# Context modulation dot products on three engines, and the second layer's gate dot products made in the second layer

## The chip, the cores and the metric

The kernel runs on one core of one Trainium2 chip. A core has a matrix engine (PE, with its weight loads shown as PEld), a vector engine (DVE), a scalar engine (ACT), a general-purpose engine (POOL) and a queue that issues the transfers (SP). Each engine takes its own instructions in the order in which the program lists them, and waits on semaphores for the others. The metric is the device time of one execution in microseconds; lower is better. About 0.3% (4.4 us) is what a measurement of this kernel can tell from no change.

## The reference

Two layers work on 1024 latent tokens and 256 context tokens of width 1024. Ahead of each layer a conditioning vector gives three vectors per token kind (shift, scale, gate), by a product with a weight matrix; the latent tokens use `c`, the context tokens use `c_ctx`:

```python
silu_c, silu_cc = silu(c), silu(c_ctx)
for i in range(2):
    shift, scale, gate = split(silu_c @ w_ada[i] + b_ada[i], 3)
    shift_c, scale_c, gate_c = split(silu_cc @ w_ada[i] + b_ada[i], 3)
    u = h * (1 + scale) + shift            # context: uc with shift_c, scale_c
    y, yc = mixer_a(u, uc) if i == 0 else mixer_b(u, uc)
    h = layer_norm(alpha * h + gate * y)   # context: hc with gate_c, first layer only
```

`mixer_a` is windowed attention of 16 heads with a sink and a SiLU gate path; `mixer_b` is a neighbourhood attention of 16 heads with a learned bias. All is float32. The context's output of the second layer is not needed, so the second layer's `gate_c` is never used.

## The kernel before

**Matrix products.** To keep float32 accuracy, every operand is split into a high part (a rounded copy, made on ACT) and a low part (the rest, made on DVE or POOL), and each product is three matmuls (L207 to L209). Weights of 128x512 come in by transfers (L149), ACT copies the high part (L163), and POOL or DVE makes the low part (L165).

**First layer, about 120 to 610 us.** The attention is cut into 160 sub-blocks (head pair p of 8, query block b of 10, head h of 2). One sub-block goes through these steps. PE makes the scores S_A (L685, L686). DVE adds the mask and takes the row maximum: s_A (L315). POOL copies the sink into one more column (L320). ACT takes the exponential and its row sum (L322). DVE inverts the sum: rs_A (L326). POOL multiplies by it (L327). PE transposes: T_A (L334). ACT copies the high part: pth_A (L338). DVE makes the low part: ptl_A (L340). PE multiplies with the values: pvA (L714). The scores run three sub-blocks ahead of the transposes. Scores and transposes take turns in the same two PSUM buffers (`big`), so PE can write the next one only when DVE has read the one that stands there: T_A waits for s_A, S_A waits for ptl_A.

Between these steps PE does the projections of the next head pair (gate and query), laid in by `merge`. Their results leave PSUM through `g_evac` (ACT L275, DVE L276) and `rope_evac` with `q_store` (DVE L463, L464, POOL L465, DVE L466, ACT L640, DVE L641). A head pair is called a unit below; the rope work falls in the second half of a unit, in its query blocks 6 to 9 (its tail), the earlier ones are its head.

**The dot products.** The modulation of the first layer's gate and of the whole second layer is 32 columns of 128 outputs, and for each the vector `silu(c)` (v=0) and, for the first 24 columns, `silu(c_ctx)` (v=1) has to be multiplied with 128 rows of `w_ada` and summed. This is spread over the first layer's attention. `dot_half(h, j)` (from L584) handles one half of the 1024 terms of column j: it loads 128x512 of `wadaT` (L597) and gives DVE a multiply-and-sum with v=1 (L600, if j < 24) and one with v=0 (L601). There are 64 such steps, laid into units 0 to 6 by `SEG` (9 or 10 a unit, every seventh item of a unit's list). With their second instruction, which reads the sum out, they are 112 dot products on DVE. `dots_end` (L604) adds the halves and the bias and forms `colA`, `colB` for the second layer's input.

**Second layer, from about 640 us.** Projections run first; the attention of 16 heads begins at 823 us, with the steps of the first layer (L1016 and L1017 for S_B, L315, L322, L326, L327, L334, L338, L340). Heads are stored to and loaded from DRAM by SP (L906, L915, L967, L972). The second layer's gate (columns 24 to 31) is used only after the attention, by `gate_rows`.

**What sets the order.** The code is recorded once; a list scheduler then places each instruction on its engine by modelled times and priorities (`tc.high_priority` lifts the attention's steps). The order on an engine can thus differ from the order in the code. Once placed, an engine never takes a later instruction ahead of one that waits.

Of the kernel before, what the change touches and what calls it, by code (L numbers as in the profile page):

```python
# [11 lines left out]
F32 = mybir.dt.float32  # L12
# [3 lines left out]
ALU = mybir.AluOpType  # L16
# [3 lines left out]
P = 128  # L20
# [17 lines left out]

SDOTS = (1, 3)

SEG = (9, 9, 9, 9, 9, 9, 10, 0)


def f32(ap):
# [38 lines left out]
def build(tc, i, out):  # L83
# [494 lines left out]
    dma(msk, i["maskA"])  # L578


    dhalf = cp.tile([P, 32, 2], F32, name="dhalf")
    gh = []

    def dot_half(h, j):  # L584
        def run():
            if j == 0:
                gh.clear()
                for v in range(2):
                    t = px.tile([P, 512], F32, tag=f"gh{v}", bufs=1, name="gh")
                    dma(t, bass.AP(i["cr"].tensor, v * D + h * 512, [[0, P], [1, 512]]))  # L590
                    th = px.tile([P, 512], F32, tag="gw", bufs=2, name="gth")
                    nc.scalar.activation(th, t, AF.Tanh, scale=0.5)
                    nc.vector.scalar_tensor_tensor(t, th, 1.0, t, ALU.add, ALU.mult)
                    gh.append(t)
            acc = dhalf if h else dcol
            t = px.tile([P, 512], F32, tag="gw", bufs=2, name="gw")
            dma(t, i["wadaT"][j, :, h * 512 : (h + 1) * 512])  # L597
            if j < 24:
                o = ap_.tile([P, 512], F32, tag="ra", bufs=1, name="gj")
                nc.vector.tensor_tensor_reduce(o, t, gh[1], 0.5, 0.0, ALU.mult, ALU.add, accum_out=acc[:, j, 1:2])  # L600
            nc.vector.tensor_tensor_reduce(t, t, gh[0], 0.5, 0.0, ALU.mult, ALU.add, accum_out=acc[:, j, 0:1])  # L601

        return (0.0, run, 0)

    def dots_end():
        for v in range(2):
            n = 24 if v else 32
            d = dcol[:, 0:n, v]
            nc.vector.tensor_tensor(d, d, dhalf[:, 0:n, v], ALU.add)
            nc.vector.tensor_tensor(d, d, bad[:, 16 : 16 + n], ALU.add)  # L610
            shift, scale = dcol[:, 8:16, v], dcol[:, 16:24, v]
            nc.vector.scalar_tensor_tensor(colA[:, v, :], scale, 1.0, lnc[:, 0, :], ALU.add, ALU.mult)
            nc.vector.scalar_tensor_tensor(colB[:, v, :], scale, 1.0, lnc[:, 1, :], ALU.add, ALU.mult)
            nc.vector.tensor_tensor(colB[:, v, :], colB[:, v, :], shift, ALU.add)

    dots = [dot_half(h, j) for h in range(2) for j in range(32)]
    evs = []
    for c, (t0, n) in enumerate(CHUNKS):
        for nt in range(2):
# [469 lines left out]
    e_load(0)  # L1089
    bias_make(0)  # L1090
    e_load(1)
    attB = [(0.0, start_B, kqv_done[0])]
    last = 0
    for n, row in enumerate(rowsB):
        ex = []
        if n < len(subsB):
            h, jp, r = subsB[n]
            if h == 14 and jp == 0 and r == 0:
                last = len(attB)
            if h + 1 < NH and r == 0:  # L1100
# [181 lines left out]
```

## Time and profile before

| what | before |
|---|---|
| median of 3 runs (lowest, highest) | 1473.45 us (1472.22, 1476.23) |
| the profiled execution | 1476.44 us, of which the span from first to last instruction is 1474.7 us |
| PE busy over the span | 1401.7 us (95%) |
| DVE busy | 1048.1 us (71%) |
| ACT busy | 715.9 us (49%) |
| POOL busy | 620.1 us (42%) |
| mean granted TensorE clock | 0.983 |

The span stands 1.7 us below the profiled execution's own time, and that execution is 3.0 us above the median. A share over the whole span hides the stages: DVE is near full in the first layer and about half full in the second, so the prediction reads the stretches apart. PE's busy time is modelled and counts overlapping matmuls once; what matters is where PE stands idle and for whom.

### The profile page before, as it was taken

What the parts mean: (1) busy time and instruction counts of PE and PEld (TensorE: products, weight loads), DVE (VectorE), ACT (ScalarE), POOL (GpSimd) and SP (SyncE); (2) the same over time, 40 slices, a digit from 0 to 9 for tenths busy, and PEclk for the clock granted to TensorE, in tenths of its full rate; (3) what the DMA queues carried; (4) which work ended last, traced back from release to release, by engine and by line L of the source; (5) the groups of instructions that cost most, each with busy time, mean ns of one, the idle gap of its engine ahead of it and who ended that gap; (6) DMA issues with size and microseconds to landing.
All of it is one profiled execution on the core that took longest, in us unless ns stands there. A gap on an engine that the chain in (4) does not pass through costs nothing.

```text
span 1474.7 us, 24806 instructions
## 1 busy us (share of the span) xinstructions
PE 1401.7 (95%) x8660; PEld 1231.5 (84%) x8660; DVE 1048.1 (71%) x2339; ACT 715.9 (49%) x1481; POOL 620.1 (42%) x739
## 2 busy tenths in 40 slices
PE   7898999999999999999999999999999999998995
PEld 5797888888888788878888889888998899877784
DVE  6957999988998988666632565655565555677788
ACT  4525566666666668633222444554454444457300
POOL 3433655555655546423311232332233323345564
PEclk6999999999999999999999999999999999999998
DMA  8455222311412213333267355555555465564443
GB/s 308 160 191 149 65 90 80 122 62 54 134 45 75 90 49 119 115 128 131 91 191 209 95 162 153 151 171 140 163 159 162 131 177 150 143 191 123 140 118 91
DMA packets 117084, 194.51 MB, mean 132 GB/s; under 512 B 9312, under 2 KB 57824, under 8 KB 116960
## 3 DMA queue, kind: packets, MB, share of 16 engines
q1 hardware_dynamic: 116960, 192.92, 43.7%
q8 instruction: 69, 1.13, 0.3%
q14 instruction: 55, 0.45, 0.1%
HBM read 140.98 MB, written 51.90 MB: 131 GB/s over the span
## 4 chain that ended last, share of the span: by engine, by line
PE 62%; DVE 19%; issue 6%; ACT 5%; DMA 4%; POOL 3%; SPq 0%; DVEq 0%; ACTq 0%; POOLq 0%
PE pj L207 8%; PE pj L209 8%; PE pj L208 8%; PE T_B L334 4%; PE pvB L1047 4%; DVE s_A L315 3%; PE T_A L334 3%; DVE ptl_A L340 3%; PE pv L240 3%; PE pv L241 3%; PE pv L242 3%; PE S_B L1016 3%; PE yA L419 2%; PE yA L417 2%; PE yA L418 2%
## 5 line engine op out<-in xcount | busy, mean ns | idle before, releaser
L327 POOL TENSOR_SCALAR s_B<-s_B,rs_B 128x640 f32<-128x640 f32 (+1 forms) x128 | 101.6, 794 | 304.0 <-DVE rs_B L326 281.2
L207 PE MATMUL pj<-uBh,wh 128*128 128x512 f32 (+1 forms) x448 | 176.2, 393 | 0.0
L322 ACT ACTIVATE s_A<-s_A,m_A 128x641 f32<-128x641 f32 (+2 forms) x160 | 119.6, 747 | 116.7 <-DVE m_A L315 94.8
L208 PE MATMUL pj<-uBl,wh 128*128 128x512 f32 (+1 forms) x448 | 169.5, 378 | 0.0
L209 PE MATMUL pj<-uBh,wl 128*128 128x512 f32 (+1 forms) x448 | 169.4, 378 | 0.0
L327 POOL TENSOR_SCALAR s_A<-s_A,rs_A 128x640 f32<-128x640 f32 (+2 forms) x160 | 137.5, 860 | 73.3 <-DVE rs_A L326 69.6
L340 DVE TENSOR_TENSOR pt_B<-T_B,pt_B 128x640 fp32r<-128x640 f32 (+1 forms) x128 | 101.0, 789 | 84.1 <-ACT pt_B L338 83.7
L322 ACT ACTIVATE s_B<-s_B,m_B 128x640 f32<-128x640 f32 (+1 forms) x128 | 102.9, 804 | 116.2 <-DVE m_B L315 114.8
L207 PE MATMUL pj<-uAh,wh 128*128 128x512 f32 (+1 forms) x384 | 141.6, 369 | 0.0
L315 DVE CUSTOM_DVE_ANT_0 s_A<-S_A,msk,nsk 128x640 f32<-128x640 f32 (+2 forms) x160 | 123.6, 773 | 22.4 <-PE S_A L686 13.7
L209 PE MATMUL pj<-uAh,wl 128*128 128x512 f32 (+1 forms) x384 | 138.3, 360 | 0.0
L208 PE MATMUL pj<-uAl,wh 128*128 128x512 f32 (+1 forms) x384 | 137.7, 359 | 0.0
L165 POOL TENSOR_TENSOR wl<-wr,wh 128x512 fp32r<-128x512 f32 x64 | 88.6, 1386 | 100.4 <-ACT wh L163 94.2
L340 DVE TENSOR_TENSOR ptl_A<-T_A,pth_A 128x640 fp32r<-128x640 f32 (+2 forms) x160 | 113.8, 711 | 6.3 <-ACT pth_A L338 3.8
L338 ACT CAST pt_B<-T_B 128x640 fp32r<-128x640 f32 (+1 forms) x128 | 84.4, 659 | 67.3 <-PE T_B L334 66.7
L334 PE MATMUL T_A<-ident,s_A 128*128 128x128 f32 x672 | 101.3, 275 | 14.0 <-DVE m_A L315 7.4
L334 PEld LDWEIGHTS T_A<-ident,s_A 128*128 128x128 f32 x672 | 78.0, 141 | 40.3 <-issue 15.2
L315 DVE CUSTOM_DVE_ANT_0 s_B<-S_B,bias 128x640 f32<-128x640 f32 (+1 forms) x128 | 100.5, 785 | 10.4 <-PE S_B L1017 9.6
L338 ACT CAST pth_A<-T_A 128x640 fp32r<-128x640 f32 (+2 forms) x160 | 96.7, 604 | 19.4 <-PE T_A L334 16.4
L209 PEld LDWEIGHTS pj<-uBh,wl 128*128 128x128 f32 x448 | 84.2, 188 | 16.7
L334 PE MATMUL T_B<-ident,s_B 128*128 128x128 f32 x608 | 88.1, 274 | 9.9 <-DVE pt_B L340 6.2
L240 PE MATMUL pv<-wh,uBh 128*128 128x256 f32 x320 | 92.1, 288 | 0.9 <-ACT wh L163 0.9
(189 smaller groups left out, 3916.5 us busy)
## 6 DMA issues: line engine op xcount, KB each, us to landing
kB<-kdB SPq DMA_DIRECT2D x64, 320.0 KB, 5.5
gw<-in_wadaT SPq DMA_DIRECT2D x64, 256.0 KB, 2.8
vdB<-st SPq DMA_DIRECT2D x20, 512.0 KB, 3.3
vB<-vdB SPq DMA_DIRECT2D x16, 640.0 KB, 4.6
kdB<-st SPq DMA_DIRECT2D x16, 512.0 KB, 2.9
qdB<-st SPq DMA_DIRECT2D x16, 512.0 KB, 3.3
qB<-qdB SPq DMA_DIRECT2D x32, 256.0 KB, 4.7
ogr<-ogd SPq DMA_DIRECT2D x28, 256.0 KB, 3.0
```

What stands on the lines that cost most here:

```text
L165: e.tensor_tensor(lo, r, f32(hi), ALU.subtract)
L207: mm(pt[:, :n], hi[:, sl], rh, start=kt == 0, stop=False)
L208: mm(pt[:, :n], hi[:, sl], rl, start=False, stop=False)
L209: mm(pt[:, :n], lo[:, sl], rh, start=False, stop=kt == KT - 1)
L240: mm(pt, lh, hi[:, sl], start=kt == 0, stop=False)
L315: nc.vector.tensor_tensor_reduce(outp, sc, in1, scale, init if init is not None else 3e38, ALU.add, ALU.min, accum_out=s.m)
L322: nc.scalar.activation(s.t[:, :n], s.t[:, :n], AF.Exp, bias=s.m, scale=-1.0, accum_out=s.sum)
L327: nc.gpsimd.tensor_scalar(s.t[:, : s.w], s.t[:, : s.w], s.rs, 1.0, ALU.mult, ALU.mult)
L334: nc.tensor.transpose(tp[:, k * P : (k + 1) * P], s.t[:, src * P : (src + 1) * P], ident)
L338: nc.scalar.copy(pt.hi[:, :n, hl, :], tv)
L340: nc.vector.tensor_tensor(pt.lo[:, :n, hl, :], tv, f32(pt.hi[:, :n, hl, :]), ALU.subtract)
L1047: mm(ov[:, :, 1], v[:, t, :], x[:, k], start=not side and k + n == 0, stop=k == 3 and n == 1)
```

## The change

`dot_half` no longer makes columns 24 to 31, so there are 48 steps, and `SEG` lays 7 (in the last unit 6) into a unit. In each step DVE makes the v=0 dot product, POOL makes the product of the v=1 half (new L607, in place in the weight tile), and ACT sums that product over the row. The sum (new L588) is written at the start of the next step's code, by `dot_sum`. The second layer's columns 24 to 31 are loaded (new L1109) and summed on DVE (new L1118) one half at a time in one buffer, `gwB`; the code lists load and dot in turn, one at each second sub-block of heads 0 to 8.

```diff
-SEG = (9, 9, 9, 9, 9, 9, 10, 0)
+SEG = (7, 7, 7, 7, 7, 7, 6, 0)
...
-    dhalf = cp.tile([P, 32, 2], F32, name="dhalf")
-    gh = []
+    dhalf = cp.tile([P, 24, 2], F32, name="dhalf")
+    gh, sums = [], []
+
+    def dot_sum():
+
+        if sums:
+            t, acc = sums.pop()
+            nc.scalar.activation(t, t, AF.Copy, scale=0.5, accum_out=acc)
 
     def dot_half(h, j):
         def run():
+            dot_sum()
             if j == 0:
...
             dma(t, i["wadaT"][j, :, h * 512 : (h + 1) * 512])
-            if j < 24:
-                o = ap_.tile([P, 512], F32, tag="ra", bufs=1, name="gj")
-                nc.vector.tensor_tensor_reduce(o, t, gh[1], 0.5, 0.0, ALU.mult, ALU.add, accum_out=acc[:, j, 1:2])
-            nc.vector.tensor_tensor_reduce(t, t, gh[0], 0.5, 0.0, ALU.mult, ALU.add, accum_out=acc[:, j, 0:1])
+            o = ap_.tile([P, 512], F32, tag="ra", bufs=1, name="gj")
+            nc.vector.tensor_tensor_reduce(o, t, gh[0], 0.5, 0.0, ALU.mult, ALU.add, accum_out=acc[:, j, 0:1])
+            nc.gpsimd.tensor_tensor(t, t, gh[1], ALU.mult)
+            sums.append((t, acc[:, j, 1:2]))
...
     def dots_end():
+        dot_sum()
...
-    dots = [dot_half(h, j) for h in range(2) for j in range(32)]
+    dots = [dot_half(h, j) for h in range(2) for j in range(24)]
...
+    gsil = bp.tile([P, D], F32, name="gsil")
+    gwB = {}
+
+    def gate_load(j, x):
+        gwB[j, x] = bp.tile([P, 512], F32, tag="gwB", bufs=1, name=f"gwB{j}_{x}")
+        if j < 0:
+            if x == 0:
+                dma(gsil, bass.AP(i["cr"].tensor, 0, [[0, P], [1, D]]))
+        else:
+            dma(gwB[j, x], i["wadaT"][24 + j][:, HALVES[x]])
+
+    def gate_dot(j, x):
+        t = gwB.pop((j, x))
+        g, acc = gsil[:, HALVES[x]], dcol[:, 24 + j, 0:1]
+        if j < 0:
+            nc.scalar.activation(t, g, AF.Tanh, scale=0.5)
+            nc.vector.scalar_tensor_tensor(g, t, 1.0, g, ALU.add, ALU.mult)
+            return
+        nc.vector.tensor_tensor_reduce(t, t, g, 0.5, acc if x else 0.0, ALU.mult, ALU.add, accum_out=acc)
+        if j == KT - 1 and x:
+            nc.vector.tensor_tensor(dcol[:, 24:32, 0], dcol[:, 24:32, 0], bad[:, 40:48], ALU.add)
+
...
+            if h <= KT and r == 1:
+                ex.append((0.0, lambda h=h, x=jp // 2, f=gate_dot if jp % 2 else gate_load: f(h - 1, x)))
```

**Place 1: ACT and DVE in unit 1, sub-blocks 27 and 28.** Sub-blocks carry their number in the names (s_A28 is the masked score of sub-block 28), and `gw` is the weight tile of a dot product. On ACT, before:

```order
L322 ACTIVATE s_A27_2141,sum_A27_2143<-s_A27_2141,m_A27_2142 128x641
L338 CAST pth_A24_2126<-T_A25_2166 128x5x128
L163 CAST wh18_2255<-wr18_1862 128x512
L322 ACTIVATE s_A28_2187,sum_A28_2189<-s_A28_2187,m_A28_2188 128x641
L338 CAST pth_A26_2210<-T_A26_2212 128x5x128
```

and on ACT now:

```order
L322 ACTIVATE s_A27_2135,sum_A27_2137<-s_A27_2135,m_A27_2136 128x641
L338 CAST pth_A24_2120<-T_A25_2160 128x5x128
L588 ACTIVATE gw_2172,dcol_73<-gw_2172 128x512
L322 ACTIVATE s_A28_2182,sum_A28_2184<-s_A28_2182,m_A28_2183 128x641
L338 CAST pth_A26_2205<-T_A26_2207 128x5x128
L163 CAST wh18_2250<-wr18_1858 128x512
```

The sum of tile gw_2172 stands on ACT ahead of the exponential of sub-block 28. On DVE, before:

```order
L326 RECIPROCAL rs_A27_2144<-sum_A27_2143 128x1
L600 ISA gj_2179,dcol_73<-gw_2177,gh_1134 128x512
L600 ISA dcol_73 128x1
L315 ISA s_A28_2187,m_A28_2188<-S_A28_2182,msk_145,nsk_146 128x640
L315 ISA m_A28_2188 128x1
L340 TENSOR_TENSOR ptl_A24_2127<-T_A25_2166,pth_A24_2126 128x5x128
L601 ISA gw_2177,dcol_73<-gw_2177,gh_1129 128x512
L601 ISA dcol_73 128x1
L326 RECIPROCAL rs_A28_2190<-sum_A28_2189 128x1
L315 ISA s_A29_2228,m_A29_2229<-S_A29_2223,msk_145,nsk_146 128x640
```

and on DVE now:

```order
L326 RECIPROCAL rs_A27_2138<-sum_A27_2137 128x1
L606 ISA gj_2174,dcol_73<-gw_2172,gh_1129 128x512
L606 ISA dcol_73 128x1
L315 ISA s_A28_2182,m_A28_2183<-S_A28_2177,msk_145,nsk_146 128x640
L315 ISA m_A28_2183 128x1
L340 TENSOR_TENSOR ptl_A24_2121<-T_A25_2160,pth_A24_2120 128x5x128
L326 RECIPROCAL rs_A28_2185<-sum_A28_2184 128x1
L315 ISA s_A29_2223,m_A29_2224<-S_A29_2218,msk_145,nsk_146 128x640
```

One of the two dot products is gone; the other (of the same tile gw_2172 that ACT sums) stands where it stood, between the two reciprocals.

**Place 2: POOL at the same sub-blocks.** Before:

```order
L320 COPY s_A28_2187<-nsk_146 128x1
L327 TENSOR_SCALAR s_A27_2141<-s_A27_2141,rs_A27_2144 128x640
L165 TENSOR_TENSOR wl18_2256<-wr18_1862,wh18_2255 128x512
L320 COPY s_A29_2228<-nsk_146 128x1
L327 TENSOR_SCALAR s_A28_2187<-s_A28_2187,rs_A28_2190 128x640
```

and now:

```order
L320 COPY s_A28_2182<-nsk_146 128x1
L327 TENSOR_SCALAR s_A27_2135<-s_A27_2135,rs_A27_2138 128x640
L607 TENSOR_TENSOR gw_2172<-gw_2172,gh_1134 128x512
L320 COPY s_A29_2223<-nsk_146 128x1
L327 TENSOR_SCALAR s_A28_2182<-s_A28_2182,rs_A28_2185 128x640
```

The product of gw_2172 stands behind the scaling of sub-block 27 and ahead of that of sub-block 28.

**Place 3: DVE and SP at the start of the second layer's attention.** `pj50` and `pj52` are projections of the second head pair, `wr` raw weights, `st` tiles on their way to DRAM, and gwB2_0 is the first half of the third gate column. On DVE, before:

```order
L905 SCALAR_TENSOR_TENSOR st_9208<-pj50_2_9183,st_9208 128x256
L914 TENSOR_TENSOR st_9249<-pj52_0_9224,st_9249 128x512
L165 TENSOR_TENSOR wl57_9287<-wr57_9222,wh57_9286 128x512
L914 TENSOR_TENSOR st_9278<-pj52_1_9253,st_9278 128x512
L315 ISA s_B0_9317,m_B0_9318<-S_B0_9312,bias0_8673 128x512
```

and now:

```order
L912 SCALAR_TENSOR_TENSOR st_9209<-pj50_2_9184,st_9209 128x256
L1118 ISA gwB1_0_10083,dcol_73<-gwB1_0_10083,gsil_8687 128x512
L1118 ISA dcol_73 128x1
L921 TENSOR_TENSOR st_9250<-pj52_0_9225,st_9250 128x512
L1118 ISA gwB1_1_10337,dcol_73<-gwB1_1_10337,gsil_8687,dcol_73 128x512
L1118 ISA dcol_73 128x1
L1118 ISA gwB2_0_10585,dcol_73<-gwB2_0_10585,gsil_8687 128x512
L1118 ISA dcol_73 128x1
L165 TENSOR_TENSOR wl57_9288<-wr57_9223,wh57_9287 128x512
L921 TENSOR_TENSOR st_9279<-pj52_1_9254,st_9279 128x512
L315 ISA s_B0_9318,m_B0_9319<-S_B0_9313,bias0_8673 128x512
```

On SP, before:

```order
L149 DMA wr57_9222<-in_wBk 128x512
L906 DMA kdB1_90<-st_9208 128x2x256
L915 DMA qdB1_82<-st_9249 128x2x512
L149 DMA wr58_9290<-in_wBq 128x512
L149 DMA wr59_9292<-in_wBq 128x512
L915 DMA qdB1_82<-st_9278 128x2x512
L149 DMA wr60_9524<-in_wBv 128x512
```

and now:

```order
L1109 DMA gwB1_1_10337<-in_wadaT 128x512
L922 DMA qdB1_82<-st_9250 128x2x512
L1109 DMA gwB2_0_10585<-in_wadaT 128x512
L149 DMA wr58_9291<-in_wBq 128x512
L1109 DMA gwB2_1_10794<-in_wadaT 128x512
L149 DMA wr59_9293<-in_wBq 128x512
L922 DMA qdB1_82<-st_9279 128x2x512
L1109 DMA gwB3_0_10981<-in_wadaT 128x512
L1109 DMA gwB3_1_11199<-in_wadaT 128x512
L1109 DMA gwB4_0_11388<-in_wadaT 128x512
```

Five gate dot products stand on DVE ahead of the first masked score s_B0, though the code lists the first of them under head 1, and the other eleven follow within the first 15 sub-blocks; on SP their loads stand between the weights' loads, each waiting for the dot product that frees the one buffer.

More of the change, by code (lines that the diff above doesn't have):

```diff
@@ L597, in run @@
             dma(t, i["wadaT"][j, :, h * 512 : (h + 1) * 512])
-            if j < 24:
-                o = ap_.tile([P, 512], F32, tag="ra", bufs=1, name="gj")
-                nc.vector.tensor_tensor_reduce(o, t, gh[1], 0.5, 0.0, ALU.mult, ALU.add, accum_out=acc[:, j, 1:2])
-            nc.vector.tensor_tensor_reduce(t, t, gh[0], 0.5, 0.0, ALU.mult, ALU.add, accum_out=acc[:, j, 0:1])
+            o = ap_.tile([P, 512], F32, tag="ra", bufs=1, name="gj")
+            nc.vector.tensor_tensor_reduce(o, t, gh[0], 0.5, 0.0, ALU.mult, ALU.add, accum_out=acc[:, j, 0:1])
+            nc.gpsimd.tensor_tensor(t, t, gh[1], ALU.mult)
+            sums.append((t, acc[:, j, 1:2]))
         return (0.0, run, 0)
     def dots_end():
+        dot_sum()
         for v in range(2):
[L607 to L610, printed above, removed]
+            d = dcol[:, 0:24, v]
+            nc.vector.tensor_tensor(d, d, dhalf[:, 0:24, v], ALU.add)
+            nc.vector.tensor_tensor(d, d, bad[:, 16:40], ALU.add)
             shift, scale = dcol[:, 8:16, v], dcol[:, 16:24, v]
```

## The prediction

> **What bounds the kernel now.** I read the busy time by stretches first, to see on which engine each stage stands.
>
> ```profile
> 120.00:523.00 403.00, 383.96 (x2455) 334.29 (x2455) 360.11 (x911) 248.82 (x533) 227.29 (x327) 1.00 0.28 87
> 523.00:557.00 34.00, 32.92 (x217) 29.38 (x218) 28.55 (x73) 20.60 (x45) 14.99 (x28) 1.00 0.10 33
> 700.00:800.00 100.00, 99.13 (x573) 86.70 (x572) 41.97 (x94) 25.11 (x45) 21.64 (x24) 1.00 0.54 161
> 1000.00:1200.00 200.00, 199.95 (x1310) 181.22 (x1309) 117.32 (x278) 97.55 (x202) 64.12 (x76) 1.00 0.54 152
> ```
>
> The columns after the length are PE, PEld, DVE, ACT and POOL busy, then clock and transfers. From 120 to 523 us, where all dot products lie, DVE is busy 89% of the time, ACT 62%, POOL 56%, yet PE is busy 95%: PE is idle for 19.0 us of 403. In the second layer PE is never idle (199.95 of 200 us) and DVE is busy 59%. So the first layer is nearly PE-bound too, and all that this change can win there lies in those 19.0 us. The waits of PE in this stretch say who causes them:
>
> ```profile
> PE S_A L685 <- DVE ptl_A L340: 5.3, 12, 1.2
> PE T_A L334 <- DVE m_A L315: 5.2, 7, 2.0
> PE T_A L334 <- POOL s_A L320: 0.3, 1, 0.3
> ```
>
> PE waits for DVE, which must empty the one PSUM buffer before PE may fill it again; it hardly waits for POOL.
>
> **The change part by part. First, what DVE is relieved of.** The prices, from the groups of this stretch and of the first 130 us:
>
> ```profile
> L601 DVE CUSTOM_DVE_ANT_0 gw<-gw,gh 128x512 f32<-128x512 f32 x64 | 50.9, 797 | 2.4 <-DMA gw<-in_wadaT 2.2
> L600 DVE CUSTOM_DVE_ANT_0 gj<-gw,gh 128x512 f32<-128x512 f32 x48 | 35.8, 745 | 0.5
> L465 POOL TENSOR_TENSOR rb<-rb,sin 128x512 f32<-128x512 f32 x12 | 15.4, 1284 | 17.2 <-DVE rb L463 17.2
> L163 ACT CAST wh<-wr 128x512 fp32r<-128x512 f32 x26 | 15.9, 613 | 8.8 <-PE pj L208 8.7
> ...
> L498 POOL TENSOR_TENSOR prod<-wada,scb 128x1024 f32<-128x1024 f32 x9 | 26.7, 2984 | 30.4 <-ACT prod L499 15.9 <-DMA wada<-in_wadaS 14.4
> L499 ACT ACTIVATE prod<-prod 128x1024 f32<-128x1024 f32 x9 | 9.5, 1055 | 2.8 <-POOL prod L498 2.8
> L499 ACT ACTIVATION_READ_ACCUMULATOR prod<-prod 128x1 f32 x9 | 1.7, 186 | 0.0
> ```
>
> The 112 dot products take 50.9 + 35.8 = 86.7 us of DVE, and 64 of them leave the first layer: about 50 us. What that is worth depends on whether PE waits behind them. The trace holds the comparison: the first 13 sub-blocks of a unit with few and with many dot products, then the last 7 of a unit with and without; the second block counts the dot instructions in three of the same stretches.
>
> ```profile
> 315.60:356.10 40.50, 39.93 (x260) 35.35 (x259) 31.30 (x74) 25.96 (x53) 19.89 (x32) 1.00 0.13 43
> 439.00:479.60 40.60, 39.76 (x261) 35.29 (x260) 36.40 (x93) 26.61 (x54) 22.95 (x32) 1.00 0.23 75
> 479.60:500.60 21.00, 19.60 (x127) 16.58 (x126) 20.24 (x53) 12.22 (x31) 12.57 (x19) 1.00 0.33 95
> 542.70:561.60 18.90, 18.58 (x126) 16.57 (x125) 14.85 (x41) 11.34 (x29) 7.79 (x17) 1.00 0.17 57
> ...
> 315.60:356.10 40.50, 3.30 (x4) 1.00 0.13 43
> 439.00:479.60 40.60, 8.64 (x12) 1.00 0.23 75
> 479.60:500.60 21.00, 5.18 (x7) 1.00 0.33 95
> ```
>
> The head of a unit takes 40.50 us with 4 dot products and 40.60 us with 12: spread out, eight of them cost PE 0.1 us. The tail takes 21.00 us with 7 and 18.90 without, but that later tail also has two fewer POOL instructions and two fewer ACT instructions, since no further weights are split there. So the relief lies between nothing and, with all 2.1 us of a tail laid to its 7 and half of them gone in six units, 6.3 us. From the other side: if the idle share of the whole stretch fell to that of the dot-free 34 us (1.08 of 34, 3.2%), 12.8 of the 19.0 us would stay, a gain of 6.2 us; 19.0 is the limit. I take -6 us.
>
> **Second, the ring.** Code and order differ. The code writes the sum one step later, but on ACT (place 1 above) the sum of tile gw_2172 stands right behind its own step, ahead of the exponential of sub-block 28. On POOL (place 2) its product stands behind the scaling of sub-block 27, which waits for that reciprocal on DVE. And on DVE the reciprocal of 28 waits for the exponential of 28. So for a part of the steps DVE, POOL, ACT and DVE wait for each other in turn. Here is the same pattern in unit 2 as it runs now: DVE, POOL, ACT and then PE.
>
> ```profile
> 255.57 0.16 DVE L326 RECIPROCAL rs_A<-sum_A 128x1 f32<-128x1 f32 x1
> 255.69 0.69 DVE L600 CUSTOM_DVE_ANT_0 gj<-gw,gh 128x512 f32<-128x512 f32 x1
> ...
> 258.32 0.16 DVE L326 RECIPROCAL rs_A<-sum_A 128x1 f32<-128x1 f32 x1
> ...
> 259.12 0.89 DVE L315 CUSTOM_DVE_ANT_0 s_A<-S_A,msk,nsk 128x640 f32<-128x640 f32 x1
> 259.93 0.08 DVE L315 DVE_READ_ACCUMULATOR2_ANT m_A<- 128x1 f32 x1
> ...
> 254.56 0.80 POOL L327 TENSOR_SCALAR s_A<-s_A,rs_A 128x640 f32<-128x640 f32 x1 [0.89 <-DVE rs_A L326]
> ...
> 255.82 1.22 POOL L327 TENSOR_SCALAR s_A<-s_A,rs_A 128x640 f32<-128x640 f32 x1 [0.33 <-DVE rs_A L326]
> ...
> 257.31 0.83 ACT L322 ACTIVATE s_A<-s_A,m_A 128x641 f32<-128x641 f32 x1 [1.40 <-DVE m_A L315]
> 258.05 0.19 ACT L322 ACTIVATION_READ_ACCUMULATOR s_A<-s_A,m_A 128x1 f32 x1
> ...
> 260.20 0.71 PE L334 MATMUL T_A<-ident,s_A 128*128 128x128 f32 x5
> ```
>
> POOL's scaling ends at 257.04. Put the product behind it: between 1.28 us (L465, the same shape) and 1.49 (half of L498), I take 1.4, to 258.5. The sum on ACT then runs from 258.6 for 0.6 (a 128x512 pass of L163) plus 0.19, to 259.4. The exponential that now starts at 257.31 starts 2.1 us later and ends at 260.4; so the reciprocal moves from 258.32 to 260.4, and the masked score behind it from 259.12 to 260.55. It ends at 261.45 and the transpose, which needs its buffer, goes from 260.20 to about 261.5: PE loses 1.3 us. In unit 1, at the instructions of place 1, there is more room:
>
> ```profile
> 205.30 1.24 POOL L327 TENSOR_SCALAR s_A<-s_A,rs_A 128x640 f32<-128x640 f32 x1 [0.47 <-DVE rs_A L326]
> ...
> 208.75 0.88 DVE L315 CUSTOM_DVE_ANT_0 s_A<-S_A,msk,nsk 128x640 f32<-128x640 f32 x1 [0.43 <-PE S_A L686]
> ...
> 210.43 0.71 PE L334 MATMUL T_A<-ident,s_A 128*128 128x128 f32 x5
> ```
>
> Scaling to 206.54, product to 208.0, sum to 208.9, exponential to 209.9, reciprocal to 210.05; the masked score moves from 208.75 to 210.05 and the transpose from 210.43 to about 211.0: 0.6 us. In the order, 18 of the 48 sums stand like this (twelve with the product behind a scaling, six with it behind a weight split, L165). At 0.7 us each, nearer to the lower of the two since some will run into a PE that waits anyway, that is 12.6 us; the bounds are 0 and 18 x 1.3 = 23.4.
>
> One thing in these rows bears on POOL: the scaling takes 0.80 us alone and 1.22 when a dot product began 0.13 us before it. The Trainium skill's page "SBUF — State Buffer" (section "Who interferes with whom") gives the rule: a VectorE instruction with two inputs in SBUF and a GpSimd instruction that reads SBUF shut each other out for the whole instruction. The trace agrees by those 0.42 us. By that rule, as an estimate from the page and L465, the 21 or so products that fall in tails could each hold up a rope addition (L466, L641) by up to 1.28 us, 27 us of DVE at most; fewer dot products would in turn free POOL.
>
> **Third, the other 30 sums and products.** Each sum is 0.8 us of ACT ahead of a pth_A or an exponential, each product 1.4 us of POOL ahead of scalings, which PE hardly waits for. Bounds 0 and 0.8 us each; nearest are the head rows above, where eight added instructions cost 0.1 us in all on a fuller engine. I take 0.1 us each, 3 us.
>
> **Fourth, the second layer.** The 16 gate dot products, two tanh and two multiplications are 16 us of DVE and ACT where PE is the bound (199.95 of 200), so their own time is hidden. But they do not wait for heads 0 to 8: they stand packed around the start of the attention (place 3), with one buffer, so each load waits on SP for the dot product before it, and DVE waits for each load. The weights' loads stand behind them on SP, and masked scores behind them on DVE. A load of this size lands in 2.8 us:
>
> ```profile
> gw<-in_wadaT SPq DMA_DIRECT2D x64, 256.0 KB, 2.8
> ```
>
> Eleven of them stand among the attention's steps; the bounds are 0 and 11 x 2.8 = 31 us. Most have two or more instructions between them, and DVE is only 42% to 59% busy there, so I take 1 us.
>
> The two half changes (the reload of `gh`) and `dots_end` stay; the last sum adds one wait of at most 2 us for `dots_end`, within the third term's bounds.
>
> **The sum.** -6 + 12.6 + 3 + 1 = +10.6 us. Against the profiled execution's own time, 1476.44, that is 1487.0; against the median of the runs, 3.0 us lower, 1473.45 + 10.6 = 1484 us.
>
> **The rivals.** *Faster: the relief counts and the ring does not close.* If the sums find their products done because ACT comes to them late (it is busy 62%, and its exponentials are queued behind transposes that wait for PE), the second term falls to nothing and the third to 1: -6 + 0 + 1 + 1 = -4, and with no cost at all -6: 1467.5 to 1469.5. For it: DVE is 89% busy and PE waits for DVE alone. Against it: the order above, in which ACT has nothing between pth_A and the sum; it decides for this rival if the median wait of those 18 sums for POOL is under some 0.3 us. The Trainium skill's page "Perfetto Trace Analysis" (section "Optimizing Scalar/DVE Operations") would point here: with DVE saturated, moving work to Scalar or even GPSIMD may pay, though it warns that between GPSIMD and DVE it might not, as they share a port. Chance 0.2.
>
> *No difference: both are small.* Heads do not feel the dot products (0.1 us for eight), and the ring costs 0.3 us each: -6 + 5.4 + 0 + 0.6 = 0, 1473.5. For it: POOL and ACT have 38% and more to spare. Chance 0.22.
>
> *Slower still, in the second layer.* DVE sits on the loads of the gate columns: if half of the eleven waits reach PE at 2.8 us, +15 on the forecast's other terms, -6 + 12.6 + 3 + 15, about 1498. Against it: the low load of DVE there. Chance 0.08.
>
> **How the numbers follow.** The forecast, slower by about 10 us through the ring, has 0.5. With the last rival, slower by over 0.3% (4.4 us, about what a measurement of this kernel can tell from no change) has 0.58, within 0.3% 0.22, faster 0.2. That the change does not do what it says is in part settled by the order: the sums do not come one dot later, and the gate dots do not spread over heads. The range reaches from 1466, a little under the faster rival, to 1497: ring at its upper bound, -6 + 23.4 + 3 + 1 = +21, is 1495, and the last rival is cut. Within the forecast alone it would be 1478 to 1495.
>
> **What would show each step right or wrong.** The dot groups on DVE fall from 112 to 48 in the first layer and 16 appear in the second, all before about 900 us. If the ring is right, L588 on ACT shows an idle time before it that is laid to POOL's L607, of 1 us or more for some 18 to 30 of 48, L326 on DVE waits for ACT's L322 far more than now, and PE's waits for s_A (L315) grow; the heads lengthen from 40.6 us to 42 or 43, while the tails shorten or stay. I am wrong if the heads stay at 40.5 us, or if L588's waits lie under 0.3 us. The fourth term is wrong if the stretch from 700 to 1000 us lengthens by more than 3 us, or if DVE's waits for gwB carry more than 5 us into PE.

## The result, and the profile after

| | before | after |
|---|---|---|
| median (lowest, highest) of 4 runs each, on one chip | 1473.88 us (1472.22, 1476.23) | 1497.01 us (1495.12, 1499.94) |
| ratio to before, 95% interval | | 1.0150 (1.0135 to 1.0165) |
| the profiled execution, its span | 1476.44, 1474.7 us | 1497.35, 1495.6 us |

The change makes the kernel 1.5% slower, 23.1 us by the medians; the forecast was 10.6 us, and the time lies just above the range. The table gives the start of single masked scores (L315) in the trace, and so where the time goes; "B0" is the first sub-block of the second layer's attention.

| | 20 | 80 | 140 | B0 | B16 | B64 | end |
|---|---|---|---|---|---|---|---|
| before, us | 182.9 | 374.0 | 556.8 | 823.2 | 884.4 | 1104.7 | 1474.7 |
| after, later by | 1.3 | 10.1 | 18.1 | 16.5 | 19.7 | 20.7 | 20.9 |

Some 17 us are lost steadily along the first layer's attention and 3 us in the first 16 sub-blocks of the second's. First the busy times by stretches: the head of unit 3 and of unit 5, the tail of unit 5, and the middle of the second layer. These are the stretches that the prediction shows as 315.60 to 356.10, 439.00 to 479.60, 479.60 to 500.60 and 1000 to 1200, with the same sub-blocks in them.

```profile
320.20:363.90 43.70, 40.70 (x260) 35.37 (x260) 33.55 (x78) 29.70 (x63) 25.77 (x36) 1.00 0.21 65
450.80:493.70 42.90, 40.72 (x259) 35.34 (x260) 31.83 (x76) 28.47 (x61) 25.27 (x36) 1.00 0.16 53
493.70:517.30 23.60, 20.10 (x128) 16.61 (x126) 18.67 (x49) 14.20 (x37) 15.80 (x22) 1.00 0.30 85
1000.00:1200.00 200.00, 199.56 (x1296) 179.06 (x1295) 117.95 (x281) 97.70 (x202) 62.35 (x74) 1.00 0.54 153
```

The heads grow from 40.5 to 42.9 and 43.7 us, and the tail from 21.0 to 23.6, yet behind PE no engine is full: DVE, busy 96% of the tail before (20.24 of 21.00 us), is at 79% now (18.67 of 23.60), and PE itself falls from 93% to 85% there. That speaks for waiting, not for too much work on some engine. Who waits for whom stands in the waits of the first layer's attention, first before (120 to 523 us), then after (120 to 542 us):

```profile
PEld T_A L334 <- POOL s_A L327: 9.5, 13, 2.5
DVE rs_A L326 <- ACT s_A L322: 8.4, 19, 1.3
...
DVE ptl_A L340 <- ACT pth_A L338: 2.8, 7, 0.9
```

```profile
ACT gw L588 <- POOL gw L607: 65.9, 39, 3.2
DVE rs_A L326 <- ACT s_A L322: 50.5, 54, 2.1
...
PEld T_A L334 <- POOL s_A L327: 25.3, 33, 1.3
...
DVE ptl_A L340 <- ACT pth_A L338: 17.5, 16, 3.1
...
PE T_A L334 <- POOL s_A L327: 10.6, 17, 0.9
...
PE S_A L692 <- DVE ptl_A L340: 8.8, 8, 1.8
```

ACT stands at the sum (L588) until POOL has made the product (L607). Behind that sum on ACT are an exponential or a pth_A; so DVE stands at the reciprocal (L326) and at ptl_A (L340), and PE at the transpose and at the next scores. PE's weight loads for the transposes waited 9.5 us for POOL's scaling before and wait 25.3 us now; the transposes themselves, which had no such wait before, wait 10.6 us. The answer for the line of the sum alone, over the whole span, counts it:

```profile
L588 ACT ACTIVATE gw<-gw x48: 617/632/636, 137.6 to 573.5; 128x512 f32<-128x512 f32 x48
...
  POOL gw L607: 70.9, 42
```

42 of the 48 sums wait, 70.9 us in all. From the trace of each sum, 27 wait 1 us or more. 26 of the 48 stand ahead of an exponential (51.6 us of the waiting), 10 ahead of a pth_A (13.6 us), the rest mostly ahead of copies out of PSUM (L730).

One such sum in unit 1, with ACT, DVE and POOL in one list:

```profile
206.97 0.69 ACT L338 CAST pth_A<-T_A 128x640 fp32r<-128x640 f32 x1
...
207.71 1.22 POOL L327 TENSOR_SCALAR s_A<-s_A,rs_A 128x640 f32<-128x640 f32 x1 [0.46 <-DVE rs_A L326]
...
208.90 1.28 POOL L607 TENSOR_TENSOR gw<-gw,gh 128x512 f32<-128x512 f32 x1
209.00 0.08 DVE L315 DVE_READ_ACCUMULATOR2_ANT m_A<- 128x1 f32 x1
...
210.22 0.63 ACT L588 ACTIVATE gw<-gw 128x512 f32<-128x512 f32 x1 [2.56 <-POOL gw L607]
...
210.85 0.82 ACT L322 ACTIVATE s_A<-s_A,m_A 128x641 f32<-128x641 f32 x1
...
211.79 0.17 DVE L326 RECIPROCAL rs_A<-sum_A 128x1 f32<-128x1 f32 x1 [1.97 <-ACT s_A L322]
...
212.05 0.80 POOL L327 TENSOR_SCALAR s_A<-s_A,rs_A 128x640 f32<-128x640 f32 x1 [1.63 <-DVE rs_A L326]
```

The row maximum of the next sub-block is ready at 209.1. Its exponential begins at 210.85, because ACT had stood at the sum since 207.7. Then DVE stands idle for 1.97 us and POOL for 1.63: a ring in which each stands idle in turn. The second place is in the tail of unit 1. Here the sum stands ahead of a pth_A, a place to which the prediction gave 0.1 us:

```profile
248.57 1.72 POOL L165 TENSOR_TENSOR wl<-wr,wh 128x512 fp32r<-128x512 f32 x1
...
250.25 1.29 POOL L607 TENSOR_TENSOR gw<-gw,gh 128x512 f32<-128x512 f32 x1
...
251.57 0.63 ACT L588 ACTIVATE gw<-gw 128x512 f32<-128x512 f32 x1 [3.20 <-POOL gw L607]
...
252.32 0.37 ACT L338 CAST pth_A<-T_A 128x256 fp32r<-128x256 f32 x1
...
252.72 0.42 DVE L340 TENSOR_TENSOR ptl_A<-T_A,pth_A 128x256 fp32r<-128x256 f32 x1 [3.11 <-ACT pth_A L338]
...
253.20 0.50 PE L692 MATMUL S_A<-kA,qA 128*128 128x256 f32 x2 [1.82 <-DVE ptl_A L340]
```

The product stands behind a weight split of 1.72 us. ACT waits 3.20 us, DVE 3.11, and PE stands idle for 1.82 us.

### The profile page after: what moved, and what is told of

It reads as the page before. It is cut to its first block, busy times and chain, and to the rows that moved or that the text cites. A ratio compares the mean times of both kernels' runs of the same rounds, so it can differ in the third digit from the quotient of the medians.

```text
span 1495.6 us, 24902 instructions
## 1 busy us (share of the span) xinstructions
PE 1403.4 (94%) x8660; PEld 1224.5 (82%) x8660; DVE 1016.5 (68%) x2246; ACT 744.5 (50%) x1579; POOL 660.5 (44%) x787
## 4 chain that ended last, share of the span: by engine, by line
PE 59%; DVE 16%; POOL 8%; issue 7%; ACT 7%; DMA 3%; DVEq 0%; ACTq 0%; POOLq 0%; SPq 0%
PE pj L209 7%; PE pj L208 7%; PE pj L207 7%; PE T_B L334 4%; PE pvB L1054 3%; PE pv L241 3%; PE pv L240 3%; PE pv L242 3%; PE T_A L334 3%; POOL gw L607 3%; POOL s_A L327 2%; PE S_B L1023 2%; PE yA L419 2%; PE yA L417 2%; PE yA L418 2%
## 5 line engine op out<-in xcount | busy, mean ns | idle before, releaser
L327 POOL TENSOR_SCALAR s_A<-s_A,rs_A 128x640 f32<-128x640 f32 (+2 forms) x160 | 127.2, 795 | 79.4 <-DVE rs_A L326 77.7
L340 DVE TENSOR_TENSOR pt_B<-T_B,pt_B 128x640 fp32r<-128x640 f32 (+1 forms) x128 | 100.8, 788 | 79.4 <-ACT pt_B L338 79.0
L315 DVE CUSTOM_DVE_ANT_0 s_A<-S_A,msk,nsk 128x640 f32<-128x640 f32 (+2 forms) x160 | 123.6, 774 | 25.3 <-PE S_A L693 13.4
L340 DVE TENSOR_TENSOR ptl_A<-T_A,pth_A 128x640 fp32r<-128x640 f32 (+2 forms) x160 | 113.9, 712 | 21.9 <-ACT pth_A L338 18.5
L315 DVE CUSTOM_DVE_ANT_0 s_B<-S_B,bias 128x640 f32<-128x640 f32 (+1 forms) x128 | 100.3, 784 | 10.1 <-PE S_B L1024 9.0
L334 PEld LDWEIGHTS T_B<-ident,s_B 128*128 128x128 f32 x608 | 69.9, 140 | 30.5 <-issue 11.8
```

Source lines behind the costliest of these rows:

```text
L315: nc.vector.tensor_tensor_reduce(outp, sc, in1, scale, init if init is not None else 3e38, ALU.add, ALU.min, accum_out=s.m)
L327: nc.gpsimd.tensor_scalar(s.t[:, : s.w], s.t[:, : s.w], s.rs, 1.0, ALU.mult, ALU.mult)
L334: nc.tensor.transpose(tp[:, k * P : (k + 1) * P], s.t[:, src * P : (src + 1) * P], ident)
L340: nc.vector.tensor_tensor(pt.lo[:, :n, hl, :], tv, f32(pt.hi[:, :n, hl, :]), ALU.subtract)
```

## The experiments

Two theories of the first layer's loss. The *wait theory*: ACT stands at sums whose product is not made yet. The *work theory*: 48 products of 1.28 us on POOL and 48 sums of 0.8 us on ACT are too much ahead of the attention's own steps there, whoever waits. Differences are given in us of 1474, from the ratios to the kernel before, which was run beside each on the same chip; the interval of a ratio is about 0.12 to 0.17% to either side, so a difference of two is uncertain by some 2 to 3 us. Compare the ratios and not the times: the kernel before took 1474.0 to 1475.5 us beside them. Each trace is a single execution, which can lie a few us from the median.

**The relief alone.**

```diff
-            nc.gpsimd.tensor_tensor(t, t, gh[1], ALU.mult)
-            sums.append((t, acc[:, j, 1:2]))
```

> This kernel is the changed one without the product on POOL (L607) and without the sum on ACT (L588): the second column of every dot product (v = 1) is left out, and its accumulators hold zero. It measures the relief of DVE by itself, with the gate dots in the second layer kept. The wait theory (the loss of the first layer, some 17 us, comes from ACT standing at the sum until POOL has made the product, 71 us of waiting in the changed kernel) and the work theory (it comes from the added work itself, 48 products of 1.28 us ahead of POOL's scalings and 48 sums of 0.8 us ahead of ACT's exponentials, whoever waits) both expect the loss of the first layer gone: 1471 to 1478 us. If the relief is worth my 6 us and the second layer costs 3.4 us, it is 1471; if the relief is worth nothing, 1477. Over 1480 would speak against both.

1466.93 us, ratio 0.9939 (0.9927 to 0.9950): 9.0 us faster than before, beyond the end that I gave it. So the relief is larger than my 6 us. With the second layer's 3.2 us (below) in it, 64 dot products fewer on DVE are worth about 12.2 us in the first layer.

**The product without the sum.**

```diff
             nc.gpsimd.tensor_tensor(t, t, gh[1], ALU.mult)
-            sums.append((t, acc[:, j, 1:2]))
```

> The changed kernel with the product on POOL (L607) but without the sum on ACT (L588): the sums of the second column (v = 1) are left out. ACT has no wait for a product, POOL has the full 48 products. The wait theory expects the time of the kernel without both within 2 us, so 1472 to 1479. The work theory, with POOL's part as the larger (PE's waits for POOL's scaling rose from about 10 to 36 us as PE and its weight loads count them), expects 8 us or more over the kernel without both: 1483 to 1492.

1471.63 us, 0.9976 (0.9963 to 0.9989): 5.5 us over the kernel without product and sum. Neither number of mine is met well: it is more than 2 us, but not the 8 of the work theory, and the kernel stays faster than before. By the two traces 2.7 us of it stand ahead of B0, where the products are, and about half of the rest comes between B0 and B16 (5.7 us lost there, 3.8 without products), so 5.5 is an upper value for the products. Where their cost can come from shows in the groups of this kernel, 120 to 540 us, DVE's dot product beside POOL's product:

```profile
L609 POOL TENSOR_TENSOR gw<-gw,gh 128x512 f32<-128x512 f32 x47 | 60.6, 1289 | 0.5
L608 DVE CUSTOM_DVE_ANT_0 gj<-gw,gh 128x512 f32<-128x512 f32 x47 | 39.4, 838 | 0.4
```

and in the kernel without products:

```profile
L608 DVE CUSTOM_DVE_ANT_0 gj<-gw,gh 128x512 f32<-128x512 f32 x47 | 34.8, 741 | 0.4
```

DVE's dot product takes 741 ns without the products and 838 with them: 47 x 0.1 = 4.6 us more of DVE. The rule that the Trainium skill gives on its page "SBUF — State Buffer" (section "Who interferes with whom"), that a VectorE instruction with two SBUF inputs and a GpSimd instruction that reads SBUF shut each other out, fits this; that these 4.6 us make the difference is not shown.

**The sum truly one step later.** In each step ACT sums the step before's product, and writes the elementwise result into the tile `o` that this step's dot product has just written, so it cannot be placed ahead of that.

```diff
-    def dot_sum():
+    def dot_sum(o):
...
-            nc.scalar.activation(t, t, AF.Copy, scale=0.5, accum_out=acc)
+            nc.scalar.activation(o, t, AF.Copy, scale=0.5, accum_out=acc)
...
-            dot_sum()
...
             nc.vector.tensor_tensor_reduce(o, t, gh[0], 0.5, 0.0, ALU.mult, ALU.add, accum_out=acc[:, j, 0:1])
+            dot_sum(o)
             nc.gpsimd.tensor_tensor(t, t, gh[1], ALU.mult)
```

> The whole change, with the sum truly one step later on ACT: in each step ACT sums the product of the step before, after this step's dot product on DVE, whose output tile it writes. The same products and the same sums, but the product is a whole step old when ACT comes to it. The wait theory expects ACT's wait for POOL to fall from 71 us to under 10 and the first layer's loss to fall by three quarters or more: 1476 to 1482. The work theory expects little gained: 1488 to 1497.

1472.14 us, 0.9985 (0.9974 to 0.9995): all of the loss and a little more is gone, with every product and sum still made. It is 24.3 us below the changed kernel (1.0150 - 0.9985). The line of the sum in this kernel (46 of the 48; the other two, the last of each half, write into `gw`):

```profile
L588 ACT ACTIVATE gj<-gw x46: 617/633/647, 138.0 to 545.9; 128x512 f32<-128x512 f32 x46
...
  DVE dhalf L607: 11.0, 15
  DVE dcol L607: 8.7, 13
  POOL gw L609: 0.6, 1
```

ACT's wait for POOL falls from 70.9 us to 0.6. ACT now waits 19.7 us for DVE's dot product, at most 1.2 at a time, and that costs little. The waits of this kernel, 120 to 542 us:

```profile
DVE rs_A L326 <- ACT s_A L322: 20.9, 44, 1.0
...
PEld T_A L334 <- POOL s_A L327: 3.9, 8, 1.1
DVE ptl_A L340 <- ACT pth_A L338: 3.0, 9, 0.6
```

They were 50.5, 25.3 and 17.5 us. The work theory falls.

**The sum without the link.** The sum is written at the end of its own step and reads `gh[0]` instead of the product. Its unused output goes into `o`, so it follows that step's dot product on DVE.

```diff
-            nc.scalar.activation(t, t, AF.Copy, scale=0.5, accum_out=acc)
+            nc.scalar.activation(o, gh[0], AF.Copy, scale=0.5, accum_out=acc)
...
-            dot_sum()
...
             sums.append((t, acc[:, j, 1:2]))
+            dot_sum(o)
```

> The changed kernel with the sum on ACT in the same place (right behind the dot product of its own step), but reading the activations tile gh[0] instead of POOL's product, so the second column's sums (v = 1) are not computed; POOL makes all 48 products as before. ACT's 48 passes stay, their wait for POOL is gone. If the waiting is the loss, this is the time of the kernel with the late sum within 3 us, 1469 to 1475. If it is the place of the sum, ahead of an exponential, that costs, waiting or not, it stays over 1480.

1469.12 us, 0.9967 (0.9954 to 0.9979), as the wait theory has it. Its sums wait 17.9 us for DVE's dot product and no longer for POOL:

```profile
L588 ACT ACTIVATE gj<-gh x48: 617/634/644, 133.5 to 543.6; 128x512 f32<-128x512 f32 x48
...
  DVE dhalf L605: 11.1, 16
  DVE dcol L605: 6.8, 10
```

The order is not the very same, since the scheduler places each version anew, but 29 of its 48 sums stand ahead of an exponential (26 in the changed kernel), and it loses nothing by that: not the place of the sum costs, but the wait for the product in it. 48 passes on ACT beside 48 products cost no more than the products alone (0.9967 against 0.9976).

**The two parts apart.** First the first part: `SEG` as before, steps for all 32 columns, nothing in the second layer.

```diff
-    dots = [dot_half(h, j) for h in range(2) for j in range(24)]
+    dots = [dot_half(h, j) for h in range(2) for j in range(32)]
```

> The first part of the change alone: product on POOL and sum on ACT as in the changed kernel for the 24 columns, but the gate dots stay in the first layer (64 steps, 9 or 10 in a unit, the last 16 of them with DVE's dot product alone), and none in the second. If the second layer's gate dots cost the 3.4 us by which the start of attention B lengthens, this is 1493 to 1495, unless the 16 dots that are back in the first layer cost as much there; if they cost nothing, 1497. Both theories of the first layer expect the same here.

1495.63 us, 1.0136 (1.0122 to 1.0150): about 2 us below the changed kernel, between the two cases. In its trace B0 comes 17.5 us late and B16 17.4: the 3 us that the changed kernel loses there are gone, and with 16 dot products back in the first layer B0 comes 1.0 us later than in the changed kernel (16.5). That is far less than the 5.5 us that they are worth below; the sums wait less here, 60.8 us for POOL against 70.9, but why is not shown. Then the second part alone:

```diff
-            nc.vector.tensor_tensor_reduce(o, t, gh[0], 0.5, 0.0, ALU.mult, ALU.add, accum_out=acc[:, j, 0:1])
-            nc.gpsimd.tensor_tensor(t, t, gh[1], ALU.mult)
-            sums.append((t, acc[:, j, 1:2]))
...
+                nc.vector.tensor_tensor_reduce(o, t, gh[1], 0.5, 0.0, ALU.mult, ALU.add, accum_out=acc[:, j, 1:2])
+            nc.vector.tensor_tensor_reduce(t, t, gh[0], 0.5, 0.0, ALU.mult, ALU.add, accum_out=acc[:, j, 0:1])
```

> The second part of the change alone: both dot products of a step on DVE as before the change, for 24 columns (48 steps), the 16 gate dots in the second layer as in the changed kernel. The relief of 16 dot products in the first layer, at the 0.2 us each that the kernel without product and sum showed (12 to 13 us for 64), is -3; the gate dots behind the start of attention B cost +3. So no change against the kernel before, 1472 to 1477. If the change's second part is a loss by itself, over 1478.

1471.03 us, 0.9980 (0.9969 to 0.9991): 2.9 us faster than before, a little better than expected. It pays 3.2 us in the second layer (11.0 us early at B0, 7.8 at B16), so 16 steps out of the first layer are worth about 6 us.

**Steps or dot products.** The kernel before, whose 16 gate steps load their column and do nothing with it: the line moves under the `if j < 24` that stands above it.

```diff
-            nc.vector.tensor_tensor_reduce(t, t, gh[0], 0.5, 0.0, ALU.mult, ALU.add, accum_out=acc[:, j, 0:1])
+                nc.vector.tensor_tensor_reduce(t, t, gh[0], 0.5, 0.0, ALU.mult, ALU.add, accum_out=acc[:, j, 0:1])
```

> The kernel before the change with its 64 steps and all 64 loads, but without the 16 gate dot products (the gate columns' sums are left out); nothing in the second layer. The second part alone gained about 10 us in the first layer by taking 16 steps out. If that is the 16 dot products on DVE, the 10 us are gained here too, with nothing paid in the second layer: 1463 to 1466. If it is the number of steps, their loads and their crowding in a unit, it stays at 1471 to 1474.

1470.14 us, 0.9963 (0.9950 to 0.9975): 5.5 us faster than before, against about 6 for the whole steps. My 10 us were read from one execution and were too high; by the medians the dot products on DVE are nearly all of it, 0.35 us each, and the loads nothing that could be told.

**The second layer.** The late sum, with the gate dots' loads left out:

```diff
-            dma(gwB[j, x], i["wadaT"][24 + j][:, HALVES[x]])
...
-        nc.vector.tensor_tensor_reduce(t, t, g, 0.5, acc if x else 0.0, ALU.mult, ALU.add, accum_out=acc)
+        nc.vector.tensor_tensor_reduce(t, gsil[:, HALVES[1 - x]], g, 0.5, acc if x else 0.0, ALU.mult, ALU.add, accum_out=acc)
```

> The kernel with the late sum, and in the second layer the 16 gate dots without the loads of their columns: each multiplies two halves of gsil instead (the gate sums are not computed), so DVE never waits for a transfer there. If the loads' waits are the cost in the second layer, the 2.9 us between the start of attention B and its sub-block 16 vanish: 1468 to 1470. If the dot products themselves cost it, 1471 to 1473.

1470.08 us, 0.9972 (0.9963 to 0.9982). From B0 to B16 it loses 0.1 us where the late sum lost 2.9. So the dot products are hidden there, and the loads with the waits for them are what costs. In the changed kernel, 700 to 1000 us:

```profile
DVE gwB L1118 <- DMA gwB<-in_wadaT: 18.1, 11, 3.5
```

Next, the second part alone with smaller pieces and two buffers, each load one piece ahead:

```diff
-        gwB[j, x] = bp.tile([P, 512], F32, tag="gwB", bufs=1, name=f"gwB{j}_{x}")
+        gwB[j, x] = bp.tile([P, 256], F32, tag="gwB", bufs=2, name=f"gwB{j}_{x}")
```

> The second part of the change alone (both dot products of a step on DVE, 48 steps), with the gate columns of the second layer loaded in 32 pieces of 128x256 into two buffers, each load issued one piece ahead of its dot product, instead of 16 of 128x512 into one. If the waits for the loads are what the second layer's dots cost (2.9 us, gone without the loads), most of it is gained over the second part alone: 1468 to 1470. If the shorter pieces only halve the transfer and double the number of waits, the time stays at 1471.

1473.64 us, 0.9990 (0.9975 to 1.0004): nothing is gained over the second part alone (0.9980). The profiled execution was the slowest of its twelve (1479.8 us), but in it, too, 2.9 us are lost from B0 to B16, and the tile's answer shows the waits:

```profile
  DMA gwB<-in_wadaT: 18.9, 15
...
DMA to landing us min/median/max: 2.2/2.7/6.3
```

Half the size lands hardly sooner (2.7 us; 2.8 for the whole in the changed kernel), so the same waiting (18.2 us in 11 waits in the second part alone) is spread over more waits. Last, the second part alone with dots that cannot come early, since each needs a tile from the ring that the heads use in turn:

```diff
+        o = bp.tile([P, 16, 31], F32, tag="er", bufs=2, name="gjB").rearrange("p a b -> p (a b)").bitcast(BF16)[:, 0:512]
-        nc.vector.tensor_tensor_reduce(t, t, g, 0.5, acc if x else 0.0, ALU.mult, ALU.add, accum_out=acc)
+        nc.vector.tensor_tensor_reduce(o, t, g, 0.5, acc if x else 0.0, ALU.mult, ALU.add, accum_out=acc)
```

> The second part of the change alone (both dot products of a step on DVE, 48 steps), with the gate dots of the second layer truly spread: each writes its unused elementwise output, as bf16, into a tile of the ring of two that holds a head's relative positions, so two dot products go with each of the first eight heads or so and a column's load has some 8 sub-blocks of time to land. If waiting for the loads is what the second layer's dots cost, DVE's 18 us of waiting there vanish and the time falls from that of the second part alone, 1471.0, by up to 2.9 us: 1468 to 1470, the fastest kernel here that computes everything. If the load of a head's relative positions now comes late, or the dots cost by their own time, 1471 to 1475.

1468.97 us, 0.9954 (0.9937 to 0.9972): 6.8 us faster than before, the lowest ratio here of a kernel that computes everything. Its interval just touches that of the second part alone (from 0.9969), so the 3.8 us between the two are likely and not certain. Its gate dots run from 799 to 1097 us instead of 795 to 871, and the answer for the tile gwB shows

```profile
  DMA gwB<-in_wadaT: 5.1, 2
```

In its trace the loss from B0 to B16 falls to 0.6 us, but to B64 it is 2.1, against 3.3 in the second part alone: spread out, a part of the cost only comes later.

**The late sum with 64 steps.** The late sum and the first part together:

```diff
+            dot_sum(o)
             if j < 24:
...
+                nc.gpsimd.tensor_tensor(t, t, gh[1], ALU.mult)
+                sums.append((t, acc[:, j, 1:2]))
```

> The late sum together with the first part alone: products on POOL and sums one step later on ACT, and the 16 gate dots on DVE in the first layer (64 steps), none in the second layer. It gives back the 2.9 us of the second layer and pays the 16 dot products in the first, at 0.2 us each 3 us: equal to the kernel with the late sum within 2 us, 1470 to 1474. If the 16 dots spread over longer segments cost nothing there, 1469.

1481.85 us, 1.0050 (1.0036 to 1.0063): a miss of 8 us or more. The line of DVE's dot product shows a wait that is 3.0 us at most, in all, in every other kernel:

```profile
  DMA gw<-in_wadaT: 12.7, 12
```

And the same without the sums:

```diff
                 nc.gpsimd.tensor_tensor(t, t, gh[1], ALU.mult)
-                sums.append((t, acc[:, j, 1:2]))
```

> The late sum with the first part alone (64 steps, 1481.9 us) without the sums on ACT (the second column's sums are left out); the products stay. There DVE stood 12.7 us at loads, because a late sum holds one of the two buffers of gw until the next step's dot product is done, and at 9 steps in a unit the load then comes too late. If that is the loss, a buffer free as soon as POOL's product is done brings it back: 1469 to 1474. If 64 steps are too many in themselves, 1478 to 1482.

1469.66 us, 0.9962 (0.9947 to 0.9977): without the sums, 13 us are gained, so it is not the number of steps. The late sum of one step ends behind the dot product of the next, and holds one of the two buffers of `gw` until then; the load for the step after that can only start there. With 7 steps in a unit there is time for it, with 9 or 10 DVE stands at the load. That this wait and nothing else of the sum makes the 13 us is the likeliest reading, and it is not shown; a third buffer would show it.

## Why the prediction was wrong

The side and the mechanism were right, the size was not: +23.1 us against +10.6. That the time came out so near the end of the range is partly luck: the relief of DVE, taken at half of what it measured, hid 6 us of the loss.

| term | predicted | measured, from which kernels |
|---|---|---|
| relief of DVE by 64 dot products | -6 (0 to -19) | -12.2: product and sum left out (-9.0), without the second layer's 3.2 |
| the ring | +12.6 (0 to 23.4) | +24.3: changed kernel less late sum, whichever sums close it |
| the other sums and products | +3 | +6.8, for all 48, with the wait gone: product 5.5 at most, sum 1.3, which is within the uncertainty of a difference |
| second layer | +1 (0 to 31) | +3.2: B0 to B16, in five traces 2.9 to 3.8, in one (product without sum) 5.7 |
| sum | +10.6 | +22.1 (ratio 1.0150 of 1474) |

**The step that failed is the line between the second and the third term**: 18 sums in the ring at 0.7 us each, and "I take 0.1 us each" for the other 30. 42 of 48 waited. To see which of them cost the time, I took for each sum how much further PE's transposes fall behind those of the kernel with the product alone, from 2 us after ACT begins to stand at the sum to the same point of the next sum:

| sums | number | waited for POOL | PE falls behind by |
|---|---|---|---|
| the kind counted: ahead of an exponential, product behind a scaling or a weight split | 19 | 42.2 us | 15.4 us |
| ahead of a pth_A, product behind a weight split | 3 | 9.6 us | 5.6 us |
| other ones ahead of an exponential, product behind a short copy (L320) | 7 | 9.4 us | 3.4 us |
| all the rest | 19 | 9.7 us | 2.3 us |

The count held for its kind (19 against 18), and its price was near (0.81 us each against 0.7). But ten sums that were given 0.1 us closed the ring too and cost 9.0 us: three ahead of a pth_A, 1.9 us each, as at 253.20 us, and seven ahead of an exponential, 0.5 us each, whose product ran right behind a short copy and still was not done when ACT came. With the late sum in place of the product alone the four numbers are 15.6, 7.7, 3.0 and -0.5. These are differences of single executions, so the shares are rough; that most of what the ring cost beyond the predicted 12.6 us stands outside the kind counted holds by both. What tells the dear sums from the cheap ones is the length of the wait: by the product alone 23.9 us of the lag stand at the 27 sums that waited 1 us or more, and 2.7 at the other 21. The prediction's own sign, an idle time of "1 us or more for some 18 to 30 of 48", was met with 27; its sum had gone by the lower end.

**First term.** "Spread out, eight of them cost PE 0.1 us" compared the head of unit 3 with the head of unit 5. Both stood in a first layer that carried 112 dot products, and other things in them differ too; which of these hid the cost stays open. Taken out of the kernel, 16 dot products give 5.5 us and 48 others (second part alone to product and sum left out) 6.0. My 6.3 us from the tails was a half of the truth; the limit of 19.0 us of idle PE held. And the tails did not "shorten or stay": 21.0 became 23.6 us.

**Third term.** Twice what I took, all of it small beside the ring. Its "scalings, which PE hardly waits for" overlooked PE's weight loads, which already waited 9.5 us for them before the change. What I weighed as an estimate, products that hold up the rope additions in the tails, doesn't show in the changed kernel: L466 takes 681 ns on the mean after and 856 before (119 to 542 us). In the kernel with the late sum it takes 958, so there it may have its price. In the kernel with the product alone it is the dot products that grew.

**Fourth term.** "Wrong if the stretch from 700 to 1000 us lengthens by more than 3 us": it did, by 3.4 us from B0 to B32 (16.5 to 19.9 us late), and by 3.1 from 740 us, where PE's products are 16.7 us late, to 1000 us. The mechanism was the one named (one buffer, DVE behind each load); 18.1 us of waiting cost 3.2.

**The rivals.** The faster one was to decide "if the median wait of those 18 sums for POOL is under some 0.3 us"; the 19 of that kind waited 1.3 to 2.6 us. Yet the kernel that it describes exists: with the sums late the ratio is 0.9985, faster by 2.2 us, though not by the 4 to 6 it was given. No difference and the second layer's rival fall with the numbers above.

**What the move from DVE is worth.** With the wait mended, moving 48 dot products to POOL and ACT brings nothing: the late sum (0.9985) equals the second part alone (0.9980), which keeps them on DVE. DVE's relief of 6.0 us is eaten by the products and sums. The Trainium skill's page "Perfetto Trace Analysis" (section "Optimizing Scalar/DVE Operations") warns that moving work between GPSIMD and DVE might not help, since they share a port. The runs agree that it did not help, with 0.7 us between the two kernels; that the port is the reason is not shown.

## What to carry to other kernels

When one operation is split over two in-order engines, count every consumer that the scheduler places right behind its producer, not only those behind a busy queue: it can wait for the whole of the producer's run, and all that stands behind it waits too. Here 42 of 48 waited, and the waits of 1 us or more carried nearly all of the loss. Code written "one step later" is no later on the engine unless some data makes it so; writing the unused output into a tile of the later step did that here, and was worth 24 us. Then look at which buffer the later consumer holds, because the next load may have to wait for it.

## What the runs showed of the hardware

- A transfer of 128x256 float32 landed in 2.7 us and one of 128x512 in 2.8 (medians of the gate loads in the kernel with pieces and in the changed kernel): to halve it bought no time. In the kernel with the gate dots spread, 128x512 took 4.5.
- DVE's two-input dot product of 128x512 took 741 ns on the mean without products on POOL and 838 with them.
- The same waiting has very different prices: 70.9 us of ACT's waits for POOL cost 24 us, 19.7 us of its waits for DVE's dot product 1.3 at most (late sum against product alone); none of the latter is longer than 1.2 us.
